# Value products and modulation products issued in a fixed order, and an empty space under the MLP's tiles kept in layer 0 only

## The chip, the cores and the metric

One core of one Trainium2 chip runs the whole program, one launch for one input. The metric is the device time of one execution in microseconds (us); lower is better. The kernel is written in a tile language: the author writes the operations in program order, a scheduler then puts every engine's instructions into one fixed list, and on the chip each engine works its list off in that order and waits where an operand is missing.

## The reference

Two layers over 256 latent and 256 context tokens of width 1024, all in float32.

```python
def rmsnorm(x, g): ...
def ada_norm(x, g, shift, scale):
    return rmsnorm(x, g) * (1 + scale[..., None, :]) + shift[..., None, :]
...
for l in range(DEPTH):                                     # DEPTH = 2
    mod  = jnp.split(silu_c  @ w_mod[l] + b_mod[l], 6, axis=-1)      # w_mod[l]: 1024 x 6144
    modc = jnp.split(silu_cc @ w_mod[l] + b_mod[l], 6, axis=-1)
    hl, hc = ada_norm(x, g_mix[l], mod[0], mod[1]), ada_norm(xc, g_mix[l], modc[0], modc[1])
    pl, pc = project(hl, ...), project(hc, ...)            # q, k, v of three head groups
    # differential attention, 6 heads: two softmaxes per head
    w = p[:, :, 0] - lam * p[:, :, 1];  o_da  = jnp.einsum('bhqk,bkhe->bqhe', w, v_da)
    # latent attention, 6 heads: one softmax per head
    p = jax.nn.softmax(s, axis=-1);     o_mla = jnp.einsum('bhqk,bkhd->bqhd', p, v_all)
    # HGRN2, 4 heads: a chunked scan in both directions
    y = jnp.concatenate([da_post(o_da, ...), o_mla, hgrn2_out(ol_hg, ...)], axis=-1)
    x = x + mod[2] * (y @ w_out[l])
    x = x + mod[5] * sqrelu_mlp(ada_norm(x, g_mlp[l], mod[3], mod[4]), w_ff1[l], w_ff2[l])
    # not in the last layer: the same for the 256 context tokens xc
return rmsnorm(x, g_final)
```

## The kernel before

Activations lie feature by token (`xT`), 512 tokens side by side, the context first. Layer 0 computes all 512 tokens; layer 1 needs queries and MLP for the 256 latent ones only, so its row tiles are `[2, 3]` where layer 0 has `[0, 1, 2, 3]` (`qtiles`). Most linear products are done three times in a split float32 (`mm3`, lines 140 to 142: high by high, low by high, high by low). Weights stream from HBM through a ring of four 128 x 1024 buffers (`raw_tile`, `bufs=4`), all loads on SP's queue.

**Modulation.** The part of the modulation of layer 0 that the first norm does not need is computed in two groups (`mod_group(0, 1)` and `mod_group(0, 2)`, line 382). Each group has eight steps k; a step loads two `raw` tiles and issues four products (line 392) whose stationary operand is the 128 x 32 tile `scm[:, k, :]` and whose four outputs are the 32-row strips j = 0 to 3 of one PSUM tile: 128 x 512 results each. A ninth step copies the tile out, transposes it (line 399) and adds the bias (`modT`, `Gm`, lines 402 to 409). These generators are the `fillers`: `fill()` advances one of them by one `yield`, and the attention loop of layer 0 calls it at 19 of its 52 rounds (line 1293); `fill_end` advances a begun group to its end. The modulation of layer 1 is made elsewhere (`mod_beside`, in the MLP of layer 0) and is not touched.

**Attention.** `layer` (line 592) pairs each step of differential attention (`da_step`) with one of latent attention (`mla_step`, line 1211), 24 pairs in layer 0 and 12 in layer 1; a pair is one head of each kind and one row tile of 128 queries. A step has three parts: A, scores (line 930 or 1225), row maximum on DVE and exponential on ACT; B, which turns the 128 x 128 probability blocks by transposing them on PE (line 907) and copies them out of PSUM (`PT` by ACT, `mPT` by ACT or DVE, line 909); C, the value products of both steps of the pair (line 1239), `nk` = 2 or 4 blocks each, and two copies on ACT (line 1242). Differential and latent products write the two 64-row halves of one PSUM tile:

```python
for j in range(nk):
    js = slice(128 * j, 128 * j + 128)
    for PT, v, c, r in ((d.PT, dav, 2 * p + 1 - h, 1 - h), (s.PT, mv, hd, h)):
        PE.matmul(op[64 * r:64 * r + 64, 0:128], v[:, j, 64 * c:64 * c + 64], PT[:, js], start=(j == 0),
                  stop=(j == nk - 1), tile_position=(0, 64 * r))
```

In each round i the loop (line 1276) emits B of step i-2, A of step i and C of step i-3. Nothing but data and buffers ties the instructions, so the scheduler may put others between the products of one C or of one modulation step. In layer 1 the queries of a new latent head pass through DVE and three operations on POOL before their first score (lines 1190 to 1193).

**After attention.** `proj_out` multiplies by `w_out` (products `mm<-yh,wh`, and so on), then the MLP opens the pool `mlp0` or `mlp1` (line 1308). Its first tile is `gap`, 128 x 920 float32, which nothing reads or writes; then come `mhh` and `mhl`, written by `Norm.gained` (lines 306 and 307) from `xT` and `Gm`, and the hidden tiles. The pool takes over the addresses of the attention's pools, closed just before.

Of the kernel before, what the change touches and what calls it, by code (L numbers as in the profile page):

```python
# [8 lines left out]
F32 = mybir.dt.float32  # L9
# [9 lines left out]
KT = 8  # L19
# [21 lines left out]
def net(ctx: ExitStack, tc, x, c, cx, c_ctx, w_mod, b_mod, g_mix, g_mlp, w_in, w_out, da_lambda, da_subln_g,  # L41
        g_cq, g_ckv, w_uq, w_ukv, hg_lb, hg_norm_g, w_ff1, w_ff2, g_final,
        k_ident, k_cos, k_sin, k_krc, k_krs, k_mask, out):
    nc = tc.nc
    V, S, G, PE = nc.vector, nc.scalar, nc.gpsimd, nc.tensor
# [6 lines left out]
    def psum(tag, shape=(128, 512)):  # L52
        return pp.tile(list(shape), F32, tag=tag, name=tag, bufs={"mm": 4, "sc": 2, "tp": 2}[tag])
# [21 lines left out]
    scm = const.tile([128, KT, 32], F32, name="scm")  # L75
# [39 lines left out]
    def raw_tile():  # L115
        return wp.tile([128, 1024], F32, tag="raw", name="raw", bufs=4)
# [262 lines left out]
    fillers = []  # L379
    started = []  # L380

    def mod_group(l, g):
        started.append(1)
        ps = psum("mm")
        for k in range(KT):
            for hf in range(2):
                raw = raw_tile()
                c0 = g * 2048 + hf * 1024
                nc.sync.dma_start(out=raw, in_=w_mod[l].rearrange("(p k) f -> p k f", k=KT)[:, k, c0:c0 + 1024])
                for q in range(2):  # L390
                    j = 2 * hf + q
                    PE.matmul(ps[32 * j:32 * j + 32, :], scm[:, k, :], raw[:, 512 * q:512 * q + 512],  # L392
                              start=(k == 0), stop=(k == KT - 1))
            yield
        sb = ap_.tile([128, 512], F32, tag="nacc", name="modsb", bufs=1)
        V.tensor_copy(out=sb, in_=ps)
        tp = psum("tp")
        for i in range(4):
            PE.transpose(tp[:, 128 * i:128 * i + 128], sb[:, 128 * i:128 * i + 128], ident)
        tv = tp.rearrange("p (i j q) -> p q j i", i=4, q=32)  # L400
        for r in range(2):
            V.tensor_add(out=modT[l][:, r, 16 * g:16 * g + 16].rearrange("p (j i) -> p j i", i=4), in0=tv[:, r],
                         in1=vT1[:, l * 48 + 16 * g:l * 48 + 16 * g + 16].rearrange("p (j i) -> p j i", i=4))
        if g != 1:
            which = 0 if g == 0 else 1
            o = 8 if g == 0 else 32
            gc = (96 if g == 0 else 112) + l * 8
            for r in range(2):
                V.scalar_tensor_tensor(out=Gm[l][:, which, r, :], in0=modT[l][:, r, o:o + 8], scalar=1.0,
                                       in1=vT1[:, gc:gc + 8], op0=ALU.add, op1=ALU.mult)  # L410
        started.pop()
        yield
# [45 lines left out]
    for t in range(4):  # L458
        xsq = st_.tile([128, 1024], F32, tag="xsq", name="xsq", bufs=2)
        S.activation(out=xsq, in_=xraw[t], func=AF.Square, accum_out=xss[:, t:t + 1])  # L460
        for hf in range(2):
            tp = psum("tp")
            for i in range(4):
                k = 4 * hf + i
# [127 lines left out]
    def layer(l):  # L592
# [609 lines left out]
        for t in range(4):  # L1202
            ps = psum("mm")
# [7 lines left out]
        def mla_step(p, h, qi, qt, res):  # L1211
            s = Step()
            hd = 2 * p + h
            nk = 2 if qt < 2 else 4
            W = 128 * nk
            q0 = 128 * qt - T0q

            def A():
                kb, qb = heads[hd]
                if "o" not in res:  # L1220
                    res["o"] = mp.tile([128, Tq], F32, tag="om", name="om", bufs=OMB)
                    res["s"] = mp.tile([128, nq, 2], F32, tag="smm", name="smm", bufs=2)
                nb = mp.tile([128, 1], F32, tag="mnb", name="mnb", bufs=3)
                ps = psum("sc")
                PE.matmul(ps[:, 0:W], qb[:, q0:q0 + 128], kb[:, 0:W], start=True, stop=True)  # L1225
                V.tensor_reduce(out=nb, in_=ps[:, 0:W], axis=AX.X, op=ALU.max, negate=True)
                s.P = mp.tile([128, 512], F32, tag="mP", name="mP", bufs=2)
                S.activation(out=s.P[:, 0:W], in_=ps[:, 0:W], func=AF.Exp, bias=nb, accum_out=res["s"][:, qi, h:h + 1])

            def B():  # L1230
                s.PT = turned(s.P, nk, mp, "mPT", S.copy if (last and qi or qi == 0) else V.tensor_copy)

            def C():
                d = s.mate
                op = psum("sc")
                for j in range(nk):
                    js = slice(128 * j, 128 * j + 128)
                    for PT, v, c, r in ((d.PT, dav, 2 * p + 1 - h, 1 - h), (s.PT, mv, hd, h)):
                        PE.matmul(op[64 * r:64 * r + 64, 0:128], v[:, j, 64 * c:64 * c + 64], PT[:, js], start=(j == 0),  # L1239
                                  stop=(j == nk - 1), tile_position=(0, 64 * r))  # L1240
                for r, o in ((1 - h, d.res["o"]), (h, res["o"])):
                    S.copy(out=o[64 * r:64 * r + 64, q0:q0 + 128], in_=op[64 * r:64 * r + 64, 0:128])

            s.A, s.B, s.C = A, B, C
            return s
# [60 lines left out]


        with tc.tile_pool(name=f"mlp{l}", bufs=1) as fp:
            fp.tile([128, 920], F32, name="gap")
            NM = Norm(l, 1, T0q, fp.tile([128, KT, 512], F32R, name="mhh"), fp.tile([128, KT, 512], F32R, name="mhl"))  # L1310
            drain(final)
            beside = None if last else mod_beside(1)
# [132 lines left out]
```

## Time and profile before

| | |
|---|---|
| median of 3 runs | 1233.94 us (1233.19 to 1235.56) |
| the profiled execution | 1233.96 us, of which the profile's span is 1232.1 us |
| PE, matrix products | 97% of the span busy, 8318 records |
| DVE / ACT / POOL | 72% / 47% / 9% busy |
| DMA | 160 MB read from HBM, 131 GB/s over the span |
| mean granted clock of TensorE | 0.993 of full speed |

PE is TensorE, DVE is VectorE, ACT is ScalarE, SP issues the loads. L1239 is line 1239 of the kernel before. A float32 product leaves two records on PE, so 64 modulation products are 128 records and 240 value products 480; a split product leaves one. The end of a matmul record is modelled and overlaps the next one, so a duration read from a record is longer than its share of PE's time; the distance from one start to the next, or a piece of the chain of waits, is the better price. The instruction `order` of an engine, where it is quoted below, tells what stands after what and no time.

### The profile page before, as it was taken

The numbers are of one execution on the slowest core, as the hardware profiler recorded it, in microseconds if no ns is written. First come the engines' busy times: TensorE is split into PE (matmuls) and PEld (weight loads), VectorE is DVE, ScalarE is ACT, GpSimd is POOL, SyncE is SP. The second block draws the span as 40 slices with busy tenths as digits, with TensorE's granted clock in tenths as the row PEclk, the third lists the DMA queues.
The fourth block names the chain that finished last, engine by engine and source line by source line (L and its number), as shares of the span: only waits on it lengthen the run. The fifth ranks groups of instructions, "written<-read, shape, count | busy, mean of one in ns | idle before, by whom it ended". The sixth has DMA issues, their size and how long they took to land.

```text
span 1232.1 us, 21466 instructions
## 1 busy us (share of the span) xinstructions
PE 1192.5 (97%) x8318; PEld 964.9 (78%) x8318; DVE 886.3 (72%) x1786; ACT 581.8 (47%) x1114; POOL 111.4 (9%) x156
## 2 busy tenths in 40 slices
PE   6999999999999999999999999999998998999997
PEld 4677888855568777878787877787986678999997
DVE  4676587767676998765778675896788868765864
ACT  3534444576664553211233332554347874644653
POOL 2200000222200100000000000230003421000000
PEclk9999999999999999999999999999999998999999
DMA  9632223456543346555555555143314404555562
GB/s 325 191 85 57 69 58 100 120 155 196 184 168 103 103 136 194 189 165 162 177 156 156 170 170 151 55 122 92 93 54 131 127 18 135 176 186 178 184 186 69
DMA packets 138199, 170.93 MB, mean 139 GB/s; under 512 B 10883, under 2 KB 116033, under 8 KB 138097
## 3 DMA queue, kind: packets, MB, share of 16 engines
q1 hardware_dynamic: 134816, 164.08, 44.1%
q0 software_dynamic: 2704, 4.94, 1.7%
q8 instruction: 66, 1.08, 0.4%
q10 hardware_dynamic: 576, 0.53, 0.1%
q14 instruction: 37, 0.30, 0.1%
HBM read 160.21 MB, written 1.05 MB: 131 GB/s over the span
## 4 chain that ended last, share of the span: by engine, by line
PE 85%; DVE 8%; ACT 3%; POOL 1%; issue 1%; DMA 1%; SPq 0%; POOLq 0%; ACTq 0%; DVEq 0%
PE mm L140 21%; PE mm L142 21%; PE mm L141 20%; PE sc L1239 3%; PE sc L1225 2%; PE mm L392 2%; PE tp L907 2%; PE mm L218 2%; PE mm L219 2%; PE mm L220 2%; DVE wl L136 1%; PE sc L797 1%; PE mm L930 1%; PE sc L768 1%; PE sc L691 1%
## 5 line engine op out<-in xcount | busy, mean ns | idle before, releaser
L135 ACT CAST wh<-raw 128x1024 fp32r<-128x1024 f32 (+2 forms) x204 | 210.7, 1034 | 278.3 <-PE mm L141 199.6
L136 DVE TENSOR_TENSOR wl<-raw,wh 128x1024 fp32r<-128x1024 f32 (+2 forms) x201 | 242.6, 1209 | 108.8 <-ACT wh L135 106.3
L140 PE MATMUL mm<-mhh,wh 128*128 128x512 f32 (+1 forms) x512 | 173.0, 338 | 0.9 <-DVE fz L336 0.9
L140 PE MATMUL mm<-fa,wh 128*128 128x512 f32 (+1 forms) x512 | 172.5, 337 | 0.0
L141 PE MATMUL mm<-fb,wh 128*128 128x512 f32 (+1 forms) x512 | 171.9, 336 | 0.0
L142 PE MATMUL mm<-fa,wl 128*128 128x512 f32 (+1 forms) x512 | 171.9, 336 | 0.0
L142 PE MATMUL mm<-mhh,wl 128*128 128x512 f32 (+1 forms) x512 | 171.4, 336 | 0.4 <-DVE wl L136 0.4
L141 PE MATMUL mm<-mhl,wh 128*128 128x512 f32 (+1 forms) x512 | 171.7, 335 | 0.0
L426 DVE SCALAR_TENSOR_TENSOR room<-raw,scm,room 128x1024 f32<-128x1024 f32 x84 | 106.4, 1287 | 57.1 <-DMA raw<-in_w_mod_dram 57.1
L140 PE MATMUL mm<-hh,wh 128*128 128x512 f32 (+1 forms) x336 | 126.5, 381 | 4.6 <-ACT hh L351 3.3
L141 PE MATMUL mm<-hl,wh 128*128 128x512 f32 (+1 forms) x336 | 127.0, 378 | 2.3 <-DVE hl L352 2.3
L142 PE MATMUL mm<-hh,wl 128*128 128x512 f32 (+1 forms) x336 | 126.6, 377 | 1.1 <-DVE wl L136 1.1
L140 PEld LDWEIGHTS mm<-mhh,wh 128*128 128x128 f32 x512 | 96.3, 188 | 14.1 <-ACT wh L135 1.7
L140 PEld LDWEIGHTS mm<-fa,wh 128*128 128x128 f32 x512 | 97.0, 190 | 12.4 <-ACT wh L135 1.7
L142 PEld LDWEIGHTS mm<-fa,wl 128*128 128x128 f32 x512 | 97.1, 190 | 10.1
L141 PEld LDWEIGHTS mm<-fb,wh 128*128 128x128 f32 x512 | 97.2, 190 | 9.9
L142 PEld LDWEIGHTS mm<-mhh,wl 128*128 128x128 f32 x512 | 96.3, 188 | 11.0 <-DVE wl L136 0.8
L141 PEld LDWEIGHTS mm<-mhl,wh 128*128 128x128 f32 x512 | 96.3, 188 | 9.6
L140 PEld LDWEIGHTS mm<-hh,wh 128*128 128x128 f32 x336 | 63.4, 190 | 15.7 <-ACT hh L351 4.1
L141 PEld LDWEIGHTS mm<-hl,wh 128*128 128x128 f32 x336 | 64.2, 191 | 13.8 <-DVE hl L352 4.0
L142 PEld LDWEIGHTS mm<-hh,wl 128*128 128x128 f32 x336 | 64.1, 191 | 13.2 <-DVE wl L136 2.0
L347 POOL TENSOR_TENSOR nt<-nt,bc 128x256 f32<-128x256 f32 x24 | 27.0, 1131 | 483.6 <-ACT bc L326 436.1
(333 smaller groups left out, 2189.6 us busy)
## 6 DMA issues: line engine op xcount, KB each, us to landing
raw<-in_w_ff_dram SPq DMA_DIRECT2D x128, 512.0 KB, 3.8
raw<-in_w_mod_dram SPq DMA_DIRECT2D x80, 512.0 KB, 3.8
raw<-in_w_in_dram SPq DMA_DIRECT2D x42, 512.0 KB, 3.8
mraw<-in_w_mod_dram SPq DMA_DIRECT2D x32, 256.0 KB, 6.1
raw<-in_w_out_dram SPq DMA_DIRECT2D x10, 512.0 KB, 3.8
raw<-in_w_in_dram SPq DMA_DIRECT2D x16, 256.0 KB, 5.3
raw<-in_w_in_dram SPq DMA_DIRECT2D x8, 384.0 KB, 3.2
K<-dah POOLq DMA_DIRECT2D x48, 64.0 KB, 2.4
```

Source lines behind the costliest of these rows:

```text
L135: S.copy(out=wh, in_=raw)
L136: (low.pop() if low else V).tensor_sub(out=wl, in0=raw, in1=wh.bitcast(F32))
L140: PE.matmul(ps, lh, rh, start=start, stop=False)
L141: PE.matmul(ps, lh, rl, start=False, stop=False)
L142: PE.matmul(ps, ll, rh, start=False, stop=stop)
L218: PE.matmul(ps, a, wh[:, k, 0:w], start=st, stop=False)
L219: PE.matmul(ps, a, wl[:, k, 0:w], start=False, stop=False)
L220: PE.matmul(ps, b, wh[:, k, 0:w], start=False, stop=sp)
L347: G.tensor_mul(out=ts, in0=ts, in1=self.bc[:, a - T0:b - T0])
L392: PE.matmul(ps[32 * j:32 * j + 32, :], scm[:, k, :], raw[:, 512 * q:512 * q + 512], start=(k == 0), stop=(k == KT - 1))
L426: V.scalar_tensor_tensor(out=acc[r], in0=raw, scalar=scm[:, k, r:r + 1], in1=acc[r], op0=ALU.mult, op1=ALU.add)
L1239: PE.matmul(op[64 * r:64 * r + 64, 0:128], v[:, j, 64 * c:64 * c + 64], PT[:, js], start=(j == 0), stop=(j == nk - 1), tile_position=(0, 6 ...
```

## The change

The products of one modulation step are issued as one list, in the order of strips 2, 3, 0, 1, tied one after the other by scheduling dependencies without a semaphore (`in_line`), and with their priority raised by 1000; the same is done to the value products of one C, with the latent product of each block first. The two loads of step k+1 are now written ahead of the products of step k, and each group has one `yield` more (ten in place of nine). `gap` is not made in layer 1, so `mhh` starts 3680 bytes per partition lower there.

```diff
--- before.py
+++ after.py
@@ -379,18 +379,30 @@
     fillers = []
     started = []
 
+    def in_line(instrs):
+
+        for a, b in zip(instrs, instrs[1:]):
+            tc.add_manual_dep(b.ins, a.ins.name, mybir.DependencyInfo(mybir.DependencyClass.NoSync,
+                                                                     mybir.DependencyReason.DATA), reason="in line")
+
     def mod_group(l, g):
         started.append(1)
         ps = psum("mm")
+
+        def load(k):
+            raws = [raw_tile() for _ in range(2)]
+            for hf in range(2):
+                c0 = g * 2048 + hf * 1024
+                nc.sync.dma_start(out=raws[hf], in_=w_mod[l].rearrange("(p k) f -> p k f", k=KT)[:, k, c0:c0 + 1024])
+            return raws
+
+        raws = load(0)
+        yield
         for k in range(KT):
-            for hf in range(2):
-                raw = raw_tile()
-                c0 = g * 2048 + hf * 1024
-                nc.sync.dma_start(out=raw, in_=w_mod[l].rearrange("(p k) f -> p k f", k=KT)[:, k, c0:c0 + 1024])
-                for q in range(2):
-                    j = 2 * hf + q
-                    PE.matmul(ps[32 * j:32 * j + 32, :], scm[:, k, :], raw[:, 512 * q:512 * q + 512],
-                              start=(k == 0), stop=(k == KT - 1))
+            now, raws = raws, load(k + 1) if k < KT - 1 else None
+            with tc.high_priority(1000):
+                in_line([PE.matmul(ps[32 * j:32 * j + 32, :], scm[:, k, :], now[j // 2][:, 512 * (j % 2):512 * (j % 2) + 512],
+                                   start=(k == 0), stop=(k == KT - 1)) for j in (2, 3, 0, 1)])
             yield
         sb = ap_.tile([128, 512], F32, tag="nacc", name="modsb", bufs=1)
         V.tensor_copy(out=sb, in_=ps)
@@ -1233,11 +1245,10 @@
             def C():
                 d = s.mate
                 op = psum("sc")
-                for j in range(nk):
-                    js = slice(128 * j, 128 * j + 128)
-                    for PT, v, c, r in ((d.PT, dav, 2 * p + 1 - h, 1 - h), (s.PT, mv, hd, h)):
-                        PE.matmul(op[64 * r:64 * r + 64, 0:128], v[:, j, 64 * c:64 * c + 64], PT[:, js], start=(j == 0),
-                                  stop=(j == nk - 1), tile_position=(0, 64 * r))
+                with tc.high_priority(1000):
+                    in_line([PE.matmul(op[64 * r:64 * r + 64, 0:128], v[:, j, 64 * c:64 * c + 64], PT[:, 128 * j:128 * j + 128],
+                                       start=(j == 0), stop=(j == nk - 1), tile_position=(0, 64 * r))
+                             for j in range(nk) for PT, v, c, r in ((s.PT, mv, hd, h), (d.PT, dav, 2 * p + 1 - h, 1 - h))])
                 for r, o in ((1 - h, d.res["o"]), (h, res["o"])):
                     S.copy(out=o[64 * r:64 * r + 64, q0:q0 + 128], in_=op[64 * r:64 * r + 64, 0:128])
 
@@ -1306,7 +1317,8 @@
 
 
         with tc.tile_pool(name=f"mlp{l}", bufs=1) as fp:
-            fp.tile([128, 920], F32, name="gap")
+            if not last:
+                fp.tile([128, 920], F32, name="gap")
             NM = Norm(l, 1, T0q, fp.tile([128, KT, 512], F32R, name="mhh"), fp.tile([128, KT, 512], F32R, name="mhl"))
             drain(final)
             beside = None if last else mod_beside(1)
```

Three places show what the scheduler makes of it. On PE in layer 0, in the first pair of heads, between the transposes of a step of four blocks (`tp<-ident,P` and `mP`), the scores of later steps (`K,Q` and `mk,mq`) and its value products, before:

```order
L907 MATMUL tp<-ident,mP 128x128 x4
L930 MATMUL mm<-K_2489,Q_2488 128x256 x2
L1239 MATMUL sc<-PT,dav 64x128
L392 MATMUL mm<-raw,scm 32x512
L907 MATMUL tp<-ident,P_2628 128x128 x2
L1239 MATMUL sc<-mPT,mv 64x128
L1239 MATMUL sc<-PT,dav 64x128
```

and the same step now:

```order
L919 MATMUL tp<-ident,P_2627 128x128 x4
L919 MATMUL tp<-ident,mP 128x128 x4
L1237 MATMUL sc<-mk_2635,mq 128x256
L942 MATMUL mm<-K_2489,Q_2488 128x256
L1249 MATMUL sc<-mPT,mv 64x128
L1249 MATMUL sc<-PT,dav 64x128
```

Six more of the last two kinds follow in turn without a break; before, the first product stood alone, with a modulation product and two transposes between it and the other seven. Just behind that place on PE, the modulation products of step k, before:

```order
L1239 MATMUL sc<-mPT,mv 64x128
L392 MATMUL mm<-raw,scm 32x512
L907 MATMUL tp<-ident,mP 128x128 x2
L1225 MATMUL sc<-mk_2635,mq 128x256
L930 MATMUL mm<-K_2489,Q_2488 128x512 x2
L392 MATMUL mm<-raw,scm 32x512 x2
L1239 MATMUL sc<-PT,dav 64x128
```

and now:

```order
L1249 MATMUL sc<-mPT,mv 64x128
L1249 MATMUL sc<-PT,dav 64x128
L404 MATMUL mm<-raw,scm 32x512 x4
L919 MATMUL tp<-ident,P_2627 128x128 x2
L919 MATMUL tp<-ident,mP 128x128 x2
L1237 MATMUL sc<-mk_2635,mq 128x512
L1249 MATMUL sc<-mPT,mv 64x128
```

The four products of a step, which were three runs of one, one and two, are one run of four. On SP's queue in layer 0, where the loads of the modulation weights (`in_w_mod_dram`) alternate with the copies that stage the queries of a later head (`Q`), before:

```order
L389 DMA raw<-in_w_mod_dram 128x1024 x5
L888 DMA Q_2898<-dah 32x512 x2
L888 DMA Q_2898<-daq 32x512 x2
L888 DMA Q_2898<-dah 32x512 x2
L389 DMA raw<-in_w_mod_dram 128x1024 x6
```

and now:

```order
L396 DMA raw<-in_w_mod_dram 128x1024 x4
L900 DMA Q_2894<-dah 32x512 x2
L900 DMA Q_2894<-daq 32x512 x2
L900 DMA Q_2894<-dah 32x512 x2
L396 DMA raw<-in_w_mod_dram 128x1024 x8
```

In the changed kernel's numbering lines 396, 404, 900, 919, 942, 1237 and 1249 are what 389, 392, 888, 907, 930, 1225 and 1239 were. The five blocks of 5, 6, 7, 4 and 10 weight loads around the four staging blocks become 4, 8, 7, 1 and 12.

## Rows read from the trace of the kernel before

**Rows 1.** The page: busy time of three engines over the span.

```profile
PE 1192.5 (97%) x8318; PEld 964.9 (78%) x8318; DVE 886.3 (72%) x1786; ACT 581.8 (47%) x1114; POOL 111.4 (9%) x156
```

**Rows 2.** Busy time by stretch: value products of layer 0, then of layer 1.

```profile
core 0: us, PE busy (x) PEld busy (x) DVE busy (x) ACT busy (x) POOL busy (x), PEclk, DMA share, GB/s
249.30:361.30 112.00, 111.86 (x738) 61.85 (x737) 79.46 (x217) 75.42 (x226) 22.43 (x39) 1.00 0.61 188
...
953.30:1012.60 59.30, 55.82 (x418) 39.55 (x417) 47.63 (x126) 47.53 (x124) 22.43 (x34) 1.00 0.26 73
```

**Rows 3.** Waits of PE and what ended them, layer 0 attention.

```profile
PE mm L140 <- ACT P L936: 0.4, 1, 0.4
```

**Rows 4.** Groups of PE instructions by line and shape, the products that the change ties.

```profile
L1239 PE MATMUL sc<-PT,dav 128*64 128x128 f32 x240 | 37.6, 284 | 0.1
L1239 PE MATMUL sc<-mPT,mv 128*64 128x128 f32 x240 | 35.0, 281 | 0.0
L392 PE MATMUL mm<-raw,scm 128*32 128x512 f32 x128 | 28.5, 605 | 0.0
```

**Rows 5.** Chain of waits, 340 to 364 us: start, us, what, records.

```profile
343.01 0.97 PE mm L392 x2
343.99 1.03 PE sc L1239 x16
345.01 0.99 PE mm L392 x6
...
349.58 0.99 PE mm L392 x8
...
351.23 0.59 PE sc L1239 x8
...
359.30 0.36 PE sc L1239 x2
...
360.33 1.02 PE sc L1239 x14
```

**Rows 6.** Timeline of PE, 252 to 262 us: start, us, instruction.

```profile
258.75 0.70 PE L1225 MATMUL sc<-mk,mq 96*128 96x256 f32 x2
259.29 0.60 PE L907 MATMUL tp<-ident,P 128*128 128x128 f32 x4
259.73 0.60 PE L907 MATMUL tp<-ident,mP 128*128 128x128 f32 x4
260.08 0.48 PE L930 MATMUL mm<-K,Q 96*128 96x256 f32 x2
```

**Rows 7.** Timeline of all engines, 300.4 to 302.8 us: transposes and the copies that follow.

```profile
300.45 0.66 PE L907 MATMUL tp<-ident,P 128*128 128x128 f32 x4
...
301.03 0.43 PE L1239 MATMUL sc<-mPT,mv 128*64 128x128 f32 x2
301.20 0.59 ACT L909 COPY PT<-tp 128x512 f32<-128x512 f32 x1 [1.63 <-PE tp L907]
...
301.40 0.66 PE L907 MATMUL tp<-ident,mP 128*128 128x128 f32 x4
...
302.09 0.69 DVE L909 COPY mPT<-tp 128x512 f32<-128x512 f32 x1 [0.57 <-PE tp L907]
```

**Rows 8.** Line 389, the modulation weight loads, by itself.

```profile
L389 SPq DMA_DIRECT2D raw<-in_w_mod_dram x32: 327/366/1850, 222.8 to 341.7; - x32
...
DMA to landing us min/median/max: 3.4/4.6/6.9
```

**Rows 9.** Waits of PE and what ended them, layer 1 attention and its end.

```profile
PE sc L1225 <- POOL mq L1193: 4.4, 5, 1.5
PE tp L901 <- DVE P L898: 4.3, 1, 4.3
```

**Rows 10.** Waits of all engines: the first writes of the MLP tiles.

```profile
ACT mhh L306 <- DVE xT L1011: 6.3, 2, 3.2
```

## Prediction

> **What bounds the kernel now.** I began with the busy times of the page, went on to busy time by stretch and to PE's waits, and ended in the chain of waits, where each run of products has its price. The reader is to see first that PE is the busy engine of the whole span, 97% against 72% for DVE [rows 1]. The change lies in two stretches. In layer 0 the value products run from 249.3 to 361.3 us, and PE is busy for 111.86 of these 112.00 us; DVE takes 79.46 and ACT 75.42 of them, at a granted clock of 1.00, the 2.4 GHz level [rows 2]. PE's waits that leave it with nothing running come to 0.4 us there [rows 3]. So what PE's list loses in layer 0, the time should lose. In layer 1 the value products run from 953.3 to 1012.6 us, PE is busy for 55.82 of 59.30 us [rows 2], and it waits: 4.4 us before five scores, until POOL has rotated the queries of a new head, and 4.3 us behind the last value products for the end of a chain on DVE [rows 9].
>
> **Price of a run.** A run is a stretch of PE's list that holds products of one of the two kinds and nothing else. For modulation products the chain shows a run of two records (one product) at 0.97 us, of six at 0.99 and of eight (all four) at 0.99 [rows 5]: the four strips of a step run beside each other, and a run costs the same whether it holds one product or four. For value products a pair, one latent and one differential, is beside itself in the same way: sixteen records (eight products) take 1.03 us, fourteen (seven) 1.02, eight (four) 0.59, and two (a single product) 0.36 [rows 5]. That is 0.36 for the first pair or half pair and 0.22 for each further one. A step cut into one and seven costs 0.36 + 1.02 = 1.38 us, an uncut one 1.02.
>
> **The change part by part.**
>
> *Modulation runs.* The instruction order has the 64 products in 27 runs before (9 of one, 6 of two, 5 of three, 7 of four) and in 18 now: one of eight, which is two steps behind each other and counts twice, eleven of four, three of three and three of one, since a tie sets an order and does not forbid that something comes between. 27 x 0.98 = 26.5 us become 19 x 0.98 = 18.6: 7.9 us less. The busy time of the group, 28.5 us [rows 4], is these 27 runs, each with its last product's modelled end on top.
>
> *Value runs.* Counted by pairs, rounded up, the 240 products stand before in 19 runs of one pair, 13 of two, 3 of three and 21 of four: 19 x 0.36 + 13 x 0.59 + 3 x 0.80 + 21 x 1.02 = 38.3 us. Now they stand in one run of one, 12 of two and 24 of four: 31.9. That is 6.4 us less, 3.1 of it in layer 0 and 3.3 in layer 1. The two groups' busy times [rows 4] add to more because the pairs overlap.
>
> *Changes of shape.* Four transposes cost 0.44 us when other transposes follow (259.29 to 259.73, [rows 6]) and 0.58 when value products do (300.45 to 301.03, [rows 7]). So a run of another shape puts 0.1 to 0.15 us on its neighbour. There are 9 modulation runs and 19 value runs fewer: 28 x 0.10 = 2.8 us less, 4.2 by the upper price; I take the lower, as two such runs are sometimes neighbours.
>
> PE's list gets 7.9 + 6.4 + 2.8 = 17.1 us shorter, some 12.7 of it in layer 0 and 4.4 in layer 1. Against that stands what the ties give back.
>
> *The wait for the turned blocks.* A step's products now need both copies at their first instruction; before, about half of the steps began with a lone differential product while the latent block was still on its way. From the start of four transposes to the end of the copy of `mPT` it takes 302.09 + 0.69 - 301.40 = 1.38 us when DVE is free [rows 7]. At the place shown in the order, the transposes (0.44), a score of 256 columns (258.75 to 259.29, 0.54 [rows 6]) and one more score stand between, 1.0 to 1.2 us: PE waits 0.2 to 0.4. Worked out like this for all 36 steps, eight come short, by 2.9 us together. Queued behind the waiting product are the transposes and scores of later steps, and ACT and DVE wait for those. I take 3.0; at best 0, as lists before had short distances too and PE still hardly waited [rows 3]; at worst one more copy of 0.59 to 0.69 stands ahead in each step, 36 x 0.64 = 23 (the first rival).
>
> *The wait for the weights.* The loads of step k+2 need the buffers of step k, and the raised priority moves the products forward to where their data is expected. On SP the staging copies of `Q` stand behind one load more or two less than before, with several rounds to spare. A load takes 0.37 us to issue and 4.6 to land (3.4 to 6.9) [rows 8], so two of them need 0.37 + 0.37 + 4.6 = 5.3 us. In PE's list, at the prices above, the distance between the runs of step k and k+2 is 5.0 to 6.2 us in five places and more in the others. I take 1.2 us; at best 0; at worst five times 6.9 + 0.7 - 5.6 = 2.0, which is 10.
>
> *Queries of a new head, layer 1.* POOL's part does not get faster, so some of what PE saves between a head's projection and its first score turns into more of the 4.4 us [rows 9]. I take 1.5; at best 0, at worst all that layer 1 saves, 4.4. The 4.3 us behind the last products stay: that chain begins with them.
>
> *The last step of group 2* comes one call later, in `fill_end`: one copy, four transposes and four small DVE operations. They stand among the first 53 of 96 products of the first half of the output projection, and the first reader, `mhh`, waits for `xT` afterwards (3.2 us at the longest, [rows 10]). Cost 0; without that cover it would be a microsecond or two.
>
> *The gap.* The order of the MLP is the same on every engine. The first writes of its tiles wait for `xT` [rows 10], not for space, and the attention's readers of that space end with the last value product. No gain and no loss, with nothing that speaks for either end.
>
> Sum: 17.1 - 3.0 - 1.2 - 1.5 = 11.4 us less. The profiled execution took 1233.96 us (1232.1 of it span), the same as the median of 1233.94: 1222.5 us.
>
> **The rivals.**
>
> *PE waits at each step's first value product.* The place is the product behind the last transposes of its step; the price is 36 times the mean wait. At 17.1 / 36 = 0.48 us the gain is gone. One more copy in front gives 0.64 and 23 us: 1240. For it: the latent block now comes first, and ACT and DVE get the same work in less time, some 80% busy in layer 0 (79.46 of 99). Against it: eight short places of 36, and 0.4 us of waits today [rows 3]. Chance 0.07.
>
> *ACT and DVE bound the steps of layer 0.* Weight loads are busy for 61.85 of 112 us, DVE for 79.46 [rows 2]. If PE's 111.86 is filled by records that merely stretch, layer 0 gains nothing and 4.4 - 1.5 = 2.9 us are left: 1231. Against it: the price of a run is the same at every occurrence to 0.02 us [rows 5], as it would not be if PE were waiting inside. Chance 0.17, half gains (1227) included. The Trainium skill, page Perfetto Trace Analysis, section Identifying the Most-Contended Engine, takes this side: TensorE is to be judged by its busy weight loads, not by its busy matmuls, and the engine with the highest occupancy comes first. By that rule the stretch would belong to DVE and the sum would be 2.9 instead of 11.4; the prices of [rows 5] let me go by PE.
>
> *The weight loads pace PE.* The products wait the longest landing in all five tight places, 10 us, and the gain shrinks to 17.1 - 10 - 4.5 = 2.6 or a little less: 1231.5, where it can hardly be told from none. For it: the priority puts them as early as it can. Chance 0.06.
>
> *The ties do not hold the products together on the chip.* The order shows 18 and 37 runs instead of 16 and 36, so little is left of this: 1234, chance 0.04.
>
> **How the numbers follow.** The forecast, 0.66, runs from 1215 (nothing given back, upper price of a change of shape, one microsecond beyond) to 1227. The range adds the second rival up to 1231.5, and leaves out 0.17 at most. About 0.2%, 2.5 us, is what a measurement of this kernel can tell from no change. Faster are the forecast and the second rival, 0.83; within it are the third and the fourth, 0.10; slower is the first, 0.07.
>
> **What would show it.** Modulation products busy for about 20 us in place of 28.5, the same price per run, the stretch of layer 0's value products at 101 us (112.0 - 12.7 + 2.0 or so) and that of layer 1 at 56 to 57, PE's share of both as it was, and everything behind as long as before. A wait of PE for `PT` or `mPT` of 10 us or more would show the first rival; DVE or ACT above 90% busy with PE below 90%, the second; waits at the modulation products for `raw`, the third. A different wait at the first writes of `mhh` in layer 1 would show that the gap was worth something.

## The result: faster by 0.55%, some six tenths of the forecast

The changed kernel takes 1227.9 us (median of six runs), the kernel before 1234.1 on the same chip: a ratio of 0.9945, with a 95% interval of 0.9929 to 0.9960. That is 4.9 to 8.8 us less, where 11.4 were forecast. The profiled execution took 1226.88 us, 1224.8 of it span.

The page and the busy time by stretch of the changed kernel, the stretches that answer to [rows 1, 2]. Line numbers have moved: L389, L392, L1193, L1225 and L1239 are now L396, L404, L1205, L1237 and L1249.

```profile
PE 1176.2 (96%) x8318; PEld 957.7 (78%) x8318; DVE 885.7 (72%) x1786; ACT 581.7 (47%) x1114; POOL 111.9 (9%) x156
```

```profile
core 0: us, PE busy (x) PEld busy (x) DVE busy (x) ACT busy (x) POOL busy (x), PEclk, DMA share, GB/s
247.50:354.10 106.60, 101.82 (x733) 59.20 (x733) 78.60 (x213) 74.51 (x225) 22.45 (x39) 0.98 0.63 198
...
325.00:330.00 5.00, 2.41 (x13) 1.44 (x13) 4.49 (x9) 3.42 (x8) 2.03 (x3) 1.00 0.84 293
330.00:335.00 5.00, 4.94 (x27) 2.11 (x28) 0.20 (x1) 0.52 (x2) 0.00 (x0) 0.66 0.40 120
...
946.90:1007.30 60.40, 53.62 (x422) 39.34 (x423) 47.39 (x127) 47.49 (x125) 22.84 (x34) 1.00 0.25 68
```

In layer 0 PE is busy for 10.0 us less than in [rows 2], but the stretch is only 5.4 shorter: PE now stands idle for 4.8 us, and the granted clock is below 1. In layer 1 PE is busy for 2.2 us less and the stretch is 1.1 *longer*. PE's groups, which answer to [rows 4], and its waits, which answer to [rows 3, 9]:

```profile
L1249 PE MATMUL sc<-PT,dav 128*64 128x128 f32 x240 | 34.7, 284 | 0.0
L1249 PE MATMUL sc<-mPT,mv 128*64 128x128 f32 x240 | 34.5, 283 | 1.3 <-DVE mPT L921 0.7 <-ACT mPT L921 0.4
L404 PE MATMUL mm<-raw,scm 128*32 128x512 f32 x128 | 20.8, 611 | 3.0 <-DMA raw<-in_w_mod_dram 3.0
```

```profile
PE sc L1237 <- POOL mq L1205: 6.8, 6, 1.4
...
PE tp L913 <- DVE P L910: 4.8, 1, 4.8
...
PE mm L404 <- DMA raw<-in_w_mod_dram: 3.0, 2, 2.6
```

The modulation products went from 28.5 to 20.8 us of busy time, as forecast. The wait for POOL's queries rose from 4.4 to 6.8, and there is a new wait of 2.6 us for modulation weights. The timeline of PE in the changed kernel shows what stands around it (start, us, instruction), and the view of line 396 from 321.3 to 321.9 us the two loads that the wait is for:

```profile
320.24 1.06 PE L404 MATMUL mm<-raw,scm 128*32 128x512 f32 x8
...
323.88 1.06 PE L404 MATMUL mm<-raw,scm 128*32 128x512 f32 x8
...
326.39 1.02 PE L1237 MATMUL sc<-mk,mq 96*128 96x512 f32 x2
330.06 1.06 PE L404 MATMUL mm<-raw,scm 128*32 128x512 f32 x6 [2.65 <-DMA raw<-in_w_mod_dram]
...
331.21 0.27 PE L1249 MATMUL sc<-mPT,mv 128*64 128x128 f32 x1
...
332.06 0.42 PE L1249 MATMUL sc<-mPT,mv 128*64 128x128 f32 x1
...
332.64 1.91 PE L404 MATMUL mm<-raw,scm 128*32 128x512 f32 x2
```

```profile
L396 SPq DMA_DIRECT2D raw<-in_w_mod_dram x2: 328/350/372, 321.3 to 321.8; - x2
...
DMA to landing us min/median/max: 7.4/7.8/8.3
```

At 320.24, 323.88 and 330.06 stand three steps of the second group, each a run of four products (eight records), the last one cut into three and one. The loads of the third are issued right behind the first, whose buffers they take, and land 7.4 and 8.3 us after their issue. PE has come to their products 6.1 us behind the first issue (326.39 + 1.02 = 327.41) and waits 2.65 us. At the median landing of the kernel before, 4.6 us [rows 8], there would have been no wait, at its longest, 6.9, one of some 1.3 us (estimates from these times). Why these two loads took so long no run shows. Then the granted clock falls to the 1.2 GHz level; a value product takes 0.42 us in place of 0.27, a modulation product 1.91 in place of 1.06. Over the 5 us from 330 the clock is 0.66, so a third of them, 1.7 us, is lost. One late pair of loads cost 4.4 us. The run of eight products, two steps behind each other, stands elsewhere, at 251.68, and the step behind it waits only 0.34 us:

```profile
262.60 1.06 PE L404 MATMUL mm<-raw,scm 128*32 128x512 f32 x8 [0.34 <-DMA raw<-in_w_mod_dram]
```

**By stage.** For every kernel run, the times between marks of its profiled execution, in us: from the start to the first value product; to the last value product of layer 0; to the first product of `ckh` in layer 1; to the last value product; and, in layer 1's MLP, from the first product of `mhh` to the last of `fa`. In brackets what was lost to the lower clock level (half the time spent there). What lies between is 22.9 to 24.0 us, and the end behind it 10.0, everywhere.

| kernel | to layer 0's | layer 0's value products | to layer 1's `ckh` | attention, layer 1 | MLP, layer 1 | ratio to before (95%) |
|---|---|---|---|---|---|---|
| before | 249.3 (3.4) | 111.8 | 577.7 | 73.7 | 186.24 | 1 |
| changed | 247.5 | 106.6 (1.7) | 577.6 | 75.7 (1.7) | 184.02 | 0.9945 (0.9929 to 0.9960) |
| e1_mod | 251.6 (6.8) | 106.6 | 576.7 | 75.3 (1.7) | 186.25 | 0.9951 (0.9934 to 0.9967) |
| e2_value | 249.5 (3.4) | 113.7 | 581.1 | 74.2 | 186.24 | 1.0037 (1.0019 to 1.0056) |
| e3_gap | 252.3 (6.8) | 111.8 | 577.8 | 76.0 (3.4) | 184.33 | 0.9984 (0.9969 to 0.9998) |
| e4_noprio | 250.4 (5.1) | 106.2 | 581.7 | 71.6 (1.7) | 185.10 | 0.9956 (0.9940 to 0.9972) |
| e5_calm | 247.4 (1.7) | 100.8 | 577.5 | 70.8 | 184.35 | 0.9888 (0.9868 to 0.9908) |
| e6_layer0 | 249.8 (5.1) | 104.0 | 577.3 | 73.7 | 184.40 | 0.9929 (0.9910 to 0.9947) |
| e7_gap408 | 252.2 (6.8) | 111.8 | 577.5 | 74.3 (1.7) | 186.23 | 1.0009 (0.9992 to 1.0026) |
| e8_nogap0 | 248.2 | 111.8 | 587.1 | 73.7 | 186.54 | 1.0093 (1.0074 to 1.0112) |
| e9_valprio | 252.1 (5.1) | 107.4 | 580.2 | 75.5 (1.7) | 184.98 | 0.9982 (0.9971 to 0.9993) |
| e10_gap664 | 249.1 (1.7) | 100.7 | 577.6 | 70.8 | 186.24 | 0.9896 (0.9878 to 0.9914) |
| e11_davfirst | 252.1 (6.8) | 106.4 | 575.8 | 73.7 | 184.33 | 0.9942 (0.9924 to 0.9960) |
| e12_gap792 | 250.5 (3.4) | 101.5 | 578.3 | 70.8 | 186.54 | 0.9900 (0.9869 to 0.9930) |

The first column is the same work in every kernel and scatters by 5 us; single profiles must therefore be compared stage by stage, less what stands in brackets. The mark behind layer 0's value products is soft: products with `w_out` stand on both sides of it, and the scheduler moves them across. Ahead of it are 15 of them before, 17 in the changed kernel, 21 in e1_mod and e11_davfirst, 13 in e5_calm, 7 in e4_noprio and 2 in e9_valprio, so the second and third columns are best read together.

### The profile page after: what moved, and what is told of

It is laid out like the page before. It is cut to its first block, busy times and chain, and to the rows that moved or that the text cites. A ratio compares the mean times of both kernels' runs of the same rounds, so it can differ in the third digit from the quotient of the medians.

```text
span 1224.8 us, 21456 instructions
## 1 busy us (share of the span) xinstructions
PE 1176.2 (96%) x8318; PEld 957.7 (78%) x8318; DVE 885.7 (72%) x1786; ACT 581.7 (47%) x1114; POOL 111.9 (9%) x156
## 5 line engine op out<-in xcount | busy, mean ns | idle before, releaser
L438 DVE SCALAR_TENSOR_TENSOR room<-raw,scm,room 128x1024 f32<-128x1024 f32 x84 | 106.4, 1287 | 56.2 <-DMA raw<-in_w_mod_dram 56.2
```

The source lines that it names most:

```text
L438: V.scalar_tensor_tensor(out=acc[r], in0=raw, scalar=scm[:, k, r:r + 1], in1=acc[r], op0=ALU.mult, op1=ALU.add)
```

## The experiments

Theory A: the runs cost what the prediction said, and what is missing was given back by waits. Rival B: ACT and DVE pace layer 0. The experiments first split the change into its three parts.

**The modulation part alone.** The new `mod_group` in the kernel before:

```diff
+            with tc.high_priority(1000):
+                in_line([PE.matmul(ps[32 * j:32 * j + 32, :], scm[:, k, :], now[j // 2][:, 512 * (j % 2):512 * (j % 2) + 512],
...
```

> Only the modulation products are tied (raised priority, loads one step ahead); value products and gap as before. In the instruction order the 64 products stand in 14 runs, two of them of eight (before: 27 runs of one to four). Theory A, a run is what costs and a late load takes some of it back: 11 runs of 0.98 us and about 0.9 us of shape changes less, 0.8 us more for value runs, so PE's list is 10.9 us shorter; behind each run of eight the next step finds no buffers loaded and costs what it cost once in the changed kernel, a wait of about 2.7 us and then about 1.6 us at the lower clock, 8.6 us for two. Net 1 to 5 us less, 1229 to 1233, waits of PE for raw of 4 us or more. Rival B, ACT and DVE pace layer 0: no change, 1234, with no waits for raw and PE's busy time as before. Rival C, late loads cost nothing, since the wait only moves: 10 us or more less, 1223.

Measured: 1228.2 against 1235.7 us, ratio 0.9951; layer 0's stretch 5.2 us shorter. The group of the modulation products fell to 16.6 us, 11.9 less than in [rows 4], and their waits for `raw` came to 2.1, with no fall of the clock in layer 0:

```profile
L404 PE MATMUL mm<-raw,scm 128*32 128x512 f32 x128 | 16.6, 603 | 2.1 <-DMA raw<-in_w_mod_dram 2.1
```

The gain is 4.1 to 8.2 us, at A's upper edge or above it, and the waits are half of A's 4 us. A's reason for them does not hold: in the trace, of the steps behind the two runs of eight (at 255.00 and 310.60) one does not wait and the other waits 0.43 us. Rival B, no change, and rival C, 10 us or more, are out.

**The value part alone**, with its raised priority:

```diff
+                with tc.high_priority(1000):
+                    in_line([PE.matmul(op[64 * r:64 * r + 64, 0:128], v[:, j, 64 * c:64 * c + 64], PT[:, 128 * j:128 * j + 128],
...
```

> Only the value products are tied, with raised priority; modulation products and gap as before. In the order the value products stand in 36 runs (32 by pairs less than before in price: 38.3 to 31.6 us), but the modulation products fall into 32 runs in place of 27. Theory A: value runs 6.7 us less, 4.9 us more for modulation runs, 1.5 us less for shape changes, 3.3 us less in all, of which some 4 us lie in layer 1; there the wait for POOL's rotated queries grows by 2 us or more and waits for the turned blocks come on top, so that layer 1 gives nothing and layer 0 little: 1233 to 1236, no change. Rival C, no give-back in layer 1: 1230 to 1231, wait for mq at 4.4 us as before.

Measured: 1.0037, slower by 2.3 to 6.9 us, more than A expected. The modulation products were broken up (group of 33.7 us, 5.2 more than before, which eats the value runs' gain), the stage behind them took 3.5 us longer, and layer 1 gained nothing, with 6.8 us of waits for `mq`:

```profile
PE sc L1231 <- POOL mq L1199: 6.8, 6, 1.4
```

**The space alone:**

```diff
-            fp.tile([128, 920], F32, name="gap")
+            if not last:
+                fp.tile([128, 920], F32, name="gap")
```

> Only the empty space below the tiles of the MLP of layer 1 is gone; products as before. Theory A: no change, 1234, and the stretch from the last value product of layer 1 to the end takes as long as before to 0.5 us. Rival D: the last 210 us of the changed kernel were 2.4 us shorter than before in its profile because of the space, so 1231.5 here.

Measured: 0.9984, an interval that just leaves out no change, and in the trace the gain that rival D named: layer 1's MLP takes 184.3 us in place of 186.2 although every engine has the same instructions in the same order. My term of zero was wrong. Busy time of this stretch, before and then here:

```profile
1035.88:1222.39 186.51, 186.41 (x1555) 185.75 (x1554) 126.39 (x236) 96.76 (x150) 0.00 (x0) 1.00 0.54 167
```

```profile
1041.37:1225.98 184.61, 184.45 (x1555) 183.75 (x1554) 126.31 (x236) 96.85 (x150) 0.00 (x0) 1.00 0.55 169
```

PE has nothing but products in both, at full clock: each product is 1% cheaper on average. The weight loads fill the stretch as well (185.75 and 183.75 us), so these rows do not tell a product's price from that of its weight load.

**Which priority does the harm.** The changed kernel raises the priority of both kinds. The next three runs take it from both, from the value products, and from the modulation products:

```diff
-            with tc.high_priority(1000):
+            if True:
                 in_line([PE.matmul(ps[32 * j:32 * j + 32, :], scm[:, k, :], now[j // 2][:, 512 * (j % 2):512 * (j % 2) + 512],
...
-                with tc.high_priority(1000):
+                if True:
                     in_line([PE.matmul(op[64 * r:64 * r + 64, 0:128], v[:, j, 64 * c:64 * c + 64], PT[:, 128 * j:128 * j + 128],
```

> The changed kernel with both ties and without the raised priority. In the order the modulation products stand in 25 runs (one of them of seven), the value products in 42 runs at 32.9 us. Theory A: 1.0 us less for modulation runs, 5.4 for value runs, 1.6 for shape changes, 8.0 us less than before in PE's list, some 4 of them in layer 1 where they are given back; few or no waits for raw and no fall of the clock in layer 0: 1229 to 1231. Rival C, no give-back in layer 1: 1226. Rival E, the priority is what brings the gain: 1234.

Measured: 0.9956, in A's range, though not in A's way: layer 1 gave nothing back. Its attention took 3.9 us less than before (lower clock left out), with 3.2 us of waits for `mq`; the stage behind layer 0's value products took 4.0 more, some 2 of them by the eight products with `w_out` that had moved into it; what the rest is stays open. Now the second hunk alone:

> The changed kernel, with the raised priority kept at the modulation products and taken from the value products, whose tie stays. In the order: 14 modulation runs (18 in the changed kernel), value runs at 34.0 us (31.9). Theory A, the raised priority of the value products puts them in front of what the next scores need, and layer 1 loses in waits for POOL what its value runs gain: the tie alone keeps the gain, as in the run without any raised priority, where layer 1's attention took 3.2 us less than before by its profile (its time at the lower clock left out) and waits for mq came to about 3 us; layer 0 gains 5 to 6 us as in the changed kernel, the MLP of layer 1 some 2 us from the space: 9 to 11 us less than before, ratio 0.991 to 0.993, and 2 to 4 us less than the changed kernel. Rival B, ACT and DVE pace layer 0 and a tie in layer 1 gives nothing whatever its priority: as the changed kernel, ratio 0.9945.

Measured: 1220.1 against 1234.5 us, ratio 0.9888, 11.4 to 16.3 us less than before and better than A expected. Layer 0's value products take 100.8 us, as long as the prediction had it, and layer 1's attention 70.8. Busy time and PE's waits:

```profile
247.40:348.30 100.90, 99.01 (x730) 59.19 (x729) 77.65 (x213) 73.66 (x225) 22.24 (x39) 1.00 0.64 205
941.40:996.50 55.10, 50.72 (x400) 36.99 (x400) 46.76 (x124) 46.40 (x122) 21.48 (x33) 1.00 0.29 81
```

```profile
PE sc L1237 <- POOL mq L1205: 3.2, 4, 1.0
...
PE mm L404 <- DMA raw<-in_w_mod_dram: 0.4, 1, 0.4
```

Nothing waits long, and no late load pulls the clock down. From e4_noprio this kernel differs by the raised priority of the modulation products alone, and that one pays: their group takes 16.6 us in place of 27.2. The first hunk alone:

> The fourth corner: as the changed kernel, but the raised priority stands at the value products alone, the modulation products are tied without it. In the order: 28 modulation runs (18 in the changed kernel, 14 in e5_calm), value runs at 31.6 us. Theory A, the raised priority of the value products breaks up the modulation products and spoils layer 1, so it costs wherever it stands: layer 0's stretch at 109 us or more, layer 1's wait for mq again near 6 us or more and its attention within 1 us of the kernel before, only the 2 us of the space left over: ratio 0.996 to 1.001. Rival H, the two priorities hurt each other and the one at the value products alone is as good as the one at the modulation products alone: ratio 0.989 to 0.991.

Measured: 0.9982, as A had it (layer 0 a little better, 107.4): the raised priority of the value products costs with or without that of the modulation products.

How it costs in layer 1 shows in ACT's timeline between a head's projection and its first score. The changed kernel, whose projection ends at 957.69, and then e5_calm, where it ends at 950.41:

```profile
957.04 0.70 ACT L948 ACTIVATE P<-mm,nb 128x512 f32<-128x512 f32 x1
...
957.72 0.59 ACT L921 COPY mPT<-tp 128x512 f32<-128x512 f32 x1
958.18 0.71 ACT L1240 ACTIVATE mP<-sc,mnb 128x512 f32<-128x512 f32 x1
...
958.86 0.58 ACT L1193 COPY mk<-mm 64x512 f32<-64x512 f32 x1
959.32 0.38 ACT L1199 COPY mq<-mm 96x256 f32<-96x256 f32 x1
```

```profile
949.54 0.59 ACT L921 COPY mPT<-tp 128x512 f32<-128x512 f32 x1
950.00 0.59 ACT L1193 COPY mk<-mm 64x512 f32<-64x512 f32 x1
950.50 0.37 ACT L1199 COPY mq<-mm 96x256 f32<-96x256 f32 x1
```

In the changed kernel two groups of transposes (from 955.71) stand inside the projection, ahead of its last products. Their copies, and the exponentials among them, come later on ACT than in e5_calm, and one exponential more (L1240) stands ahead of `mk` and `mq`: `mq` is copied 1.63 us behind the projection, against 0.09. POOL begins that much later, and PE waits 1.38 us at the score (963.44) against 0.48 (954.87). The same shows at the fifth of the six heads, where ACT has a copy of `mPT` and an operation for `yh` more ahead of `mq`: it is copied 1.38 us behind the projection against 0.59, and PE waits 1.17 us against none. These two heads make 2.1 of the 3.6 us by which the two kernels differ. At the fourth and the last head the waits grow as well (1.16 us against 0.80, 1.04 against none); ACT's list just ahead of `mq` is the same at the one, and the copy is no later behind the projection at the other, so why they grow is open. The wait for `mq` is 6.8 us in all three kernels with raised value products in layer 1 (the changed one, e2_value, e9_valprio), 4.3 or 4.4 with the old order there, or the old order within a pair (before, e1_mod, e6_layer0; e11_davfirst), and 3.2 where they are tied, latent product first, without it (e4_noprio, e5_calm).

**The value tie in layer 0 only.** Layer 1's value products as before the change:

```diff
+                if not last:
...
+                else:
+                    for j in range(nk):
+                        js = slice(128 * j, 128 * j + 128)
+                        for PT, v, c, r in ((d.PT, dav, 2 * p + 1 - h, 1 - h), (s.PT, mv, hd, h)):
```

> The changed kernel with the value products of layer 1 in the order of the kernel before (no tie, no raised priority there); layer 0 is the changed kernel's on every engine. Theory A, the value tie of layer 1 gives 3.3 us of runs and loses them in waits: the same time as the changed kernel to 1 us, ratio 0.9935 to 0.9955, with waits for mq back at about 4.4 us from 6.8 and none longer at mPT. Rival C, the tie in layer 1 did bring its 3 us and layer 0 alone was over-priced: 3 us slower than the changed kernel, ratio 0.997.

Measured: 0.9929, with an interval that overlaps A's range and leaves out C's 0.997; layer 1's attention is at 73.7 us again, the wait for `mq` at 4.3. The tie in layer 1, as the change makes it, gains nothing. Layer 0 has the changed kernel's order on every engine, and took 104.0 us in place of 106.6: the same step waited 1.72 us for its weights instead of 2.65, as the later of its two loads landed 7.3 us after its issue and not 8.3, and the clock stayed up.

**The order of a pair.** In e5_calm:

```diff
-                             for j in range(nk) for PT, v, c, r in ((s.PT, mv, hd, h), (d.PT, dav, 2 * p + 1 - h, 1 - h))])
+                             for j in range(nk) for PT, v, c, r in ((d.PT, dav, 2 * p + 1 - h, 1 - h), (s.PT, mv, hd, h))])
```

> e5_calm with the differential product ahead of the latent one in each pair, as in the kernel before; the tie stays, without raised priority. In the order the value products stand as if there were no tie: 22 runs of one pair (4 in e5_calm), 39.1 us in place of 34.0. Theory A, the runs are what costs, and putting the later block first is what holds a step's products together: about 5 us of value runs and 1 us of shape changes dearer than e5_calm, ratio 0.993 to 0.995, with the waits of PE for PT and mPT no shorter than there. Rival B, the value runs do not pay, only the modulation runs do: as e5_calm, ratio 0.989.

Measured: 0.9942, in A's range. Layer 0 with the stage behind it is 3.8 us dearer than in e5_calm (5.5 in its own stretch, into which eight products with `w_out` have moved, and 1.7 less behind it), layer 1 2.9 us. In one thing A was wrong: PE's waits for `mPT` are shorter here, none against 0.9 us; those for `raw` are longer, 1.9 against 0.4, and so not all of layer 0's loss is the value runs'. With the differential block first, a step begins before the latent block is turned, and the tie holds nothing together. With the latent block first it does, and PE's waits for it are 0.9 us in e5_calm.

**The space.** Four runs put layer 1's MLP tiles at other places, or take the space from layer 0. In the kernel before:

```diff
-            fp.tile([128, 920], F32, name="gap")
+            fp.tile([128, 408 if last else 920], F32, name="gap")
```

> The kernel before, with the space below the tiles of layer 1's MLP cut from 920 to 408 columns (the same instructions in the same order on every engine; mhh, mhl, fa and fb 2048 bytes lower). Theory F, the price of a product depends on where its moving tile lies against the weights, and 920 columns put mhh at the weights' own place modulo 4096 bytes: start to start of layer 1's MLP products differs from the 118 to 120 ns of before, and from its first product to its last takes 1 to 2 us less than 186.2 us. Theory G, what counts is only that the space is gone: 186.2 us as before.

Measured: 186.23 us as before. Theory G's number, but e3_gap's gain says that not every place is alike. In the kernel before, the space kept in layer 1 alone:

```diff
-            fp.tile([128, 920], F32, name="gap")
+            if last:
+                fp.tile([128, 920], F32, name="gap")
```

> The kernel before, with the empty space gone in layer 0 and kept in layer 1 (the same instructions in the same order on every engine). Theory F: layer 0's MLP products, 512 columns each, start at other distances than before; whether longer or shorter is open, and the size is of the order of 1% of some 370 us, 2 to 6 us either way, slower if the space stands there for this. Theory G: no change, ratio 1.000.

Measured: 1.0093, 9.1 to 13.8 us slower. The MLP of layer 0 before, and then here, the same instructions in the same order:

```profile
403.40:771.70 368.30, 365.74 (x1643) 294.32 (x1642) 271.87 (x348) 127.81 (x191) 6.71 (x8) 1.00 0.53 160
```

```profile
402.31:780.03 377.72, 376.18 (x1643) 295.44 (x1642) 273.93 (x348) 130.22 (x191) 6.74 (x8) 1.00 0.52 156
```

So the place of the tiles matters to products of 512 columns too, by 2.6%, more than theory F's 2 to 6 us, and the other way round. It is the products themselves that got dearer, not waits between them: the median distance from one start to the next goes from 227 to 234 ns. In e5_calm, two more places for layer 1:

```diff
-            if not last:
-                fp.tile([128, 920], F32, name="gap")
+            fp.tile([128, 664 if last else 920], F32, name="gap")
```

> e5_calm with an empty space of 664 columns in layer 1, so that mhh, mhl, fa and fb lie 1024 bytes lower than in the kernel before and 2656 higher than in e5_calm; the same instructions in the same order on every engine. In the runs so far 3680 bytes lower took 2 us off layer 1's MLP and 2048 lower took nothing. Theory F1, only the place modulo 1024 bytes counts: first to last product of the MLP 186.2 us, ratio 0.990 to 0.991. Theory F2, modulo 2048: another rate, with a gain or a loss of 1 to 4 us against e5_calm's 184.35.

Measured: 186.24 us, and 0.9896: F1. And with 792 in place of 664:

> e5_calm with an empty space of 792 columns in layer 1: mhh, mhl, fa and fb half a kilobyte off the places at which the MLP took 186.2 us (0, 1024 and 2048 bytes lower than in the kernel before), where e5_calm stands 416 bytes off and takes 184.35. The same instructions in the same order on every engine. Theory F1, the distance to the nearest multiple of 1024 bytes sets the price: 184.0 to 184.5 or a little less, the same time as e5_calm (ratio 0.987 to 0.991). Rival G1, e5_calm's rate comes from something else than that distance: 186.2.

Measured: 186.54 us, so F1 falls with the rival's number. Places 0, 512, 1024 and 2048 bytes below the old one cost 186.2 to 186.5 us, the place 3680 bytes below (7 times 512, and 96) costs 184.0 to 185.1. The 186.54 is no sign of the place, since in e8_nogap0, where layer 1's tiles lie at the old one, the MLP takes as long. That a place off the multiples of 512 is what layer 1 wants fits all of these, but only one such place was run, so the rule stays open.

## Why the prediction was right, and where its size was not

**Bound: right.** PE's list sets layer 0's time: in e5_calm it takes 100.8 us with PE busy for 99.01 of 100.90 and DVE for 77.65. The second rival falls with that. By the rule of the Trainium skill, page Perfetto Trace Analysis, section Identifying the Most-Contended Engine, DVE (77.65) and not PE (weight loads 59.19) would have been the engine to look at; the runs do not agree, the time went with the list of products.

**Price of a run: right.** 27 runs made 28.5 us of busy time [rows 4]; 14 runs, two of them of eight, make 16.6 (e1_mod, e5_calm). In the changed kernel 7.9 us were to go, and 7.7 went (28.5 to 20.8), the slow product at 332.64 included. The fourth rival, ties that do not hold, falls with that.

**PE's list: 12.7 us forecast for layer 0, 11.7 measured** (10.0 less busy time, 1.7 of lower clock on top). **In layer 1 4.4 forecast, 2.2 measured** in the stretch; four more products with `w_out` moved into it (55 against 51 before, 0.12 us each from start to start), so about 2.7. What is left over, 1.0 and 1.7, is about the size of the changes of shape, 2.8 us: no run shows them paid back.

**The wait for the turned blocks: over-sized.** 3.0 us were taken, and waits for `mPT` are 1.3 us. The first rival (17 us) falls.

**The wait for the weights: the step that failed in layer 0.** 1.2 us were taken: two loads need 5.3 us, at a landing of 4.6, and the tight places leave 5.0 to 6.2. The places were counted rightly: from the end of the run at 320.24 (1.0 us long) to 327.41 it is 6.2. The landing was not: the later of the two loads took 8.3 us, more than the 6.9 of the worst case too. The waits came to 3.0 (2.65 here, 0.34 behind the run of eight), and the fall of the clock added 1.7, for which the sum had no term. Together 4.7 of the 10 that the range allowed (third rival).

**Queries of a new head: under-sized, and for another reason.** 1.5 us were taken, on the view that POOL's part just stays as long while PE gets faster. The wait grew by 2.4, since the raised priority also put more of ACT's work ahead of the copy of `mq`, by transposes inside the projection (two of the six heads; the share of two others is open). The tie without raised priority makes the wait *shorter* than before, 3.2 us. With that, layer 1's attention as a whole gained nothing (73.7 before, 74.0 after less the lower clock), where 2 us or so had been counted on.

**The gap: wrong.** 0 us were taken, as no order moves and no wait ends there. The place of the tiles by itself is worth 1.9 us in layer 1 (e3_gap), 2.2 in the changed kernel and 1.1 to 2.2 over all runs that have it. The sign that was named for it, another wait at the first writes of `mhh`, did not show (6.3 us in two waits before and after): the gain lies in the products.

**The tail of group 2 and the end of layer 1's attention: right.** The stage with the tail took 577.6 us against 577.7; the wait behind the last value products stayed (4.8 us against 4.3).

So of the change's own parts layer 0 gained 5.2 us in the profile (7.8 where the clock stayed up, e6_layer0), layer 1's attention nothing, and its MLP 2.2: 7.4 us, or 10 without that fall of the clock, against 4.9 to 8.8 measured. The forecast's 11.4 needed the list to be paid out in both layers, and e5_calm, which does that, gains 13.8, 1.9 of them by the space. It beats both kernels, by the change's own ties with one line taken back.

That the measured time lies within the range is in part luck. 1227.9 is just above the forecast's own part, 1215 to 1227, in the part that was added for the second rival, and that rival's mechanism is not what happened. And 2.2 us of the gain come from the space, which the sum had at nothing; without them the time would have been about 1230.

## What to carry to other kernels

Tying products that run beside each other pays what the start-to-start distances of their runs say; put the operand that comes last first in the tie, so that the group starts once and whole. Be wary of raising the priority of a group whose inputs come from a chain through other engines: here it pulled that chain's transposes and copies ahead of work on which a longer chain depends, and the order on another engine (ACT's, one place ahead of POOL) showed it. The distance that a load has must be checked against a landing longer than any seen so far, not a usual one, with the fall of the clock behind a wait added to its price.

## What the runs showed of the hardware

- The place of a tile in on-chip memory changes the price of a product, with the same instructions in the same order on every engine: 1% for products of 256 columns (186.24 against 184.33 us), 2.6% for products of 512 columns (368.30 against 377.72), and a space that helps the one hurts the other.
- The later of two weight loads of 512 KB, issued at the same place of the program, landed after 8.3 us in the changed kernel and after 7.3 in e6_layer0; in the kernel before none of the 32 took more than 6.9 [rows 8]. PE's wait follows it (2.65 and 1.72 us).
- After PE had stood still for 2.65 us in a stretch that was otherwise full, the granted clock fell from the 2.4 to the 1.2 GHz level and cost another 1.7 us; after a wait of 1.72 us at the same instruction (e6_layer0) it did not.
- The first 250 us, the same work in all runs, lost 0 to 6.8 us to the lower clock from one profile to the next, as much as the whole effect that was to be measured.
